# A decoder layer on one core: VectorE takes fourteen weight splits from GpSimd while it works on a small matrix inverse, and the table of delays that sets TensorE's order gets values for single steps

## The chip, the cores and the metric

The kernel runs on one core of a Trainium2 chip. The metric is the device time of one execution in microseconds (us). Engines are named as the profile names them: PE is TensorE, DVE is VectorE, ACT is ScalarE, POOL is GpSimd, SP is SyncE, the engine that here issues most of the transfers.

## The reference, cut to what matters

One decoder layer on x of 512 x 1024 in float32. All products are computed to float32 accuracy.

```python
h = rms_norm(x, pre_mix_norm)
proj = h @ w_in                      # 1024 -> 3600 columns: att q,k,v; gdn q,k,v,z,a,b
o_att = moba_attention(att_q, att_k, att_v, rel_bias)      # 8 heads of 64
# gated_deltanet: 8 heads, chunks of 64; q, k, v go through a causal conv of width 4 and silu
m = where(strict, (k_beta @ k.T) * decay, 0); a_mat = m + eye(64)
u, w = triangular_solve(a_mat, [v * beta, k_beta * exp(g_cum)])
def step(state, ...):                # lax.scan over the 8 chunks
    v_new = u_c - w_c @ state
    o = q_c @ state + attn_intra @ v_new
    state = state * exp(g_last) + k_c.T @ v_new
x = x + rms_norm(concat(o_att, o_gdn) @ w_out, post_mix_norm)
h = rms_norm(x, pre_mlp_norm)
x = x + rms_norm(square(relu(h @ w_up)) @ w_down, post_mlp_norm)
```

## The kernel before

Every large product is made of three: an operand is split into a high part (a cast to the type that PE multiplies at full rate) and a low part (operand minus high part), and hi·hi, hi·lo and lo·hi are added in PSUM (`mm3`). A weight of the input projection is handled in pieces of 128 x 512, two to a group of 128 output columns. For a piece, SP issues the load into `w_raw` (two buffers), ACT casts it to `w_hi` (three buffers), and POOL subtracts, which gives `w_lo` (three buffers): `begun` and `ended`, lines 128 to 140. A `w_raw` is free again when its `w_lo` is made, a `w_hi` when PE has used it.

`ORDER` lists the groups of columns: x, y are attention's queries and keys, w its values, k, q, v, z those of the delta net. A group takes 24 products of 128 x 512 (two pieces, four times three products each) into one of two PSUM banks named `ps_mm`; then its take-over starts (`take_k`, `take_q`, `take_v`, `take_z`, `take_a`), which evicts the bank on ACT and DVE. For a v group it is one ACT instruction, three DVE instructions `conv` at L395, a tanh (`th`), the product `vt` at L399, four transposes on PE and two DVE products into `vB`. A group's bank is free after its third `conv`. This text numbers the pieces as the program does: v0 has pieces 26 and 27, v1 28 and 29, v2 30 and 31, v3 32 and 33, y1 34 and 35, x2 36 and 37, y2 38 and 39, x3 40 and 41. By this time PE also does parts of the attention: scores of a pair of heads (`ps_a<-pt`), transposes (`ps_a<-ident,L`) and products with the values (`ps_a<-ph,V`).

`inverse` (L753 to L773) inverts the 32 x 32 diagonal blocks of all chunks on DVE: 31 steps of two instructions each, `pr` (L766) and `inv` (L767), each step on the result of the one before, then a copy (L770). The result goes through DRAM: `d_u<-inv` and `d_t<-inv` write it, and `scan` (L776 on) loads it in another layout, `uap<-d_t` and `UT<-d_u`, after POOL has set `UT` to zero (L778). Two products with 32 x 32 tiles follow (`ps_g<-uap,NT` and `ps_g<-UT,uap`), then `UT,kB`, and then the eight steps of the scan.

Tiles named "big" share 14 slots. A new one gets a slot that came free, and its first writer waits for the slot's last user. `UT`, `inv` and the scores' operands `pt` are such tiles.

What sets the order: each part of the work is a Python generator. `Weave` runs them against a clock of its own that counts the products' time alone; a generator that has to wait for other engines yields a delay, or marks a name with a delay, and the delays stand in the table `WAIT`, found by the kind of the wait. So `WAIT`, with ranks (`RANK`) and a few starting times (`START`), decides in which order PE's instructions are written, and PE runs them in that order. The instructions of ACT, DVE, POOL and SP are put in order when the program is built, by a scheduler with a model of the engines. On the chip each engine and each queue then runs its list strictly in order.

## Time and profile before

| | |
|---|---|
| runs | 653.94 us median of 3 (653.29 to 654.62) |
| the profiled execution | 652.92 us, of it 651.1 us from the first to the last instruction |
| granted TensorE clock, mean | 0.985 |
| PE busy | 629.3 us (97%), 4359 instructions |
| DVE busy | 444.7 us (68%) |
| ACT busy | 359.9 us (55%) |
| POOL busy | 181.8 us (28%) |
| DMA | 113.16 MB, mean 174 GB/s |

The profiled execution is 1.02 us under the median of the runs shown. PE is said to be busy nearly all the time, but a product that runs at half clock counts as busy as well, so the rows of the granted clock have to be read beside the busy time. Up to about 270 us the kernel is the mixer (norm, projections, attention, delta net), then come the output projection and, from about 350 us, the MLP.

### The profile page before, as it was taken

What the parts mean: (1) busy time and instruction counts of PE and PEld (TensorE: products, weight loads), DVE (VectorE), ACT (ScalarE), POOL (GpSimd) and SP (SyncE); (2) the same over time, 40 slices, a digit from 0 to 9 for tenths busy, and PEclk for the clock granted to TensorE, in tenths of its full rate; (3) what the DMA queues carried; (4) which work ended last, traced back from release to release, by engine and by line L of the source; (5) the groups of instructions that cost most, each with busy time, mean ns of one, the idle gap of its engine ahead of it and who ended that gap; (6) DMA issues with size and microseconds to landing.
All of it is one profiled execution on the core that took longest, in us unless ns stands there. A gap on an engine that the chain in (4) does not pass through costs nothing.

```text
span 651.1 us, 11131 instructions
## 1 busy us (share of the span) xinstructions
PE 629.3 (97%) x4359; PEld 528.7 (81%) x4359; DVE 444.7 (68%) x619; ACT 359.9 (55%) x610; POOL 181.8 (28%) x219
## 2 busy tenths in 40 slices
PE   8999999997979999999999999999999999999995
PEld 7788787865856777688898899999998888887884
DVE  5557656698432365576664578887879888988776
ACT  6456675333364647654433576666565656665661
POOL 4465574423452333202402112311111330000002
PEclk9999999998997999999999999999999999999999
DMA  7232332413250211382368989899999999957503
GB/s 238 84 102 78 82 111 68 130 64 129 78 116 21 66 34 67 132 295 84 122 227 264 254 230 264 215 254 284 256 230 347 313 293 290 308 201 292 199 1 129
DMA packets 60341, 113.16 MB, mean 174 GB/s; under 512 B 15702, under 2 KB 34777, under 8 KB 59906
## 3 DMA queue, kind: packets, MB, share of 16 engines
q1 hardware_dynamic: 42594, 83.10, 36.6%
q0 software_dynamic: 17696, 29.36, 21.4%
q8 instruction: 34, 0.56, 0.3%
q14 instruction: 17, 0.14, 0.1%
HBM read 106.65 MB, written 35.15 MB: 218 GB/s over the span
## 4 chain that ended last, share of the span: by engine, by line
PE 82%; DVE 9%; POOL 2%; DMA 2%; ACT 2%; issue 1%; SPq 1%; DVEq 0%; POOLq 0%; ACTq 0%
PE ps_mm L80 41%; PE ps_g L80 24%; PE ps_a L80 14%; DVE inv L767 2%; DVE pr L766 2%; PE ps_a L84 1%; PE ps_g L84 1%; DMA wo_raw<-in_w_out 1%; DVE conv L395 1%; DMA xx<-in_x 1%; DMA UT<-d_u 1%; POOL w_lo L138 1%; DVE ma_l L114 0%; DVE xs L1021 0%; SPq L786 0%
## 5 line engine op out<-in xcount | busy, mean ns | idle before, releaser
L138 POOL TENSOR_TENSOR w_lo<-w_raw,w_hi 128x512 fp32r<-128x512 f32 x54 | 71.0, 1316 | 100.3 <-ACT w_hi L137 92.5
L113 ACT CAST wdh<-wd 128x1024 fp32r<-128x1024 f32 x53 | 55.9, 1054 | 52.0 <-PE ps_mm L80 23.5
L80 PE MATMUL ps_mm<-hT_h,w_hi 128*128 128x512 f32 (+1 forms) x192 | 79.8, 415 | 4.5 <-DVE conv L395 4.5
L114 DVE TENSOR_TENSOR u_l<-w,u_h 128x1024 fp32r<-128x1024 f32 x46 | 56.2, 1224 | 37.9 <-ACT u_h L113 37.9
L114 DVE TENSOR_TENSOR wdl<-wd,wdh 128x1024 fp32r<-128x1024 f32 x53 | 64.9, 1224 | 22.8 <-ACT wdh L113 22.7
L113 ACT CAST u_h<-w 128x1024 fp32r<-128x1024 f32 x46 | 47.9, 1046 | 57.1 <-PE ps_a L80 20.9
L80 PE MATMUL ps_mm<-hT_l,w_hi 128*128 128x512 f32 (+1 forms) x192 | 74.7, 389 | 0.3 <-DVE hT_l L114 0.3
L80 PE MATMUL ps_mm<-hT_h,w_lo 128*128 128x512 f32 (+1 forms) x192 | 74.4, 388 | 0.0
L1192 POOL DMA_DIRECT2D d_T<-in_w_down x32 | 33.1, 1044 | 147.4 <-DMA d_T<-in_w_down 94.2
L137 ACT CAST w_hi<-w_raw 128x512 fp32r<-128x512 f32 x56 | 34.7, 619 | 52.3 <-PE ps_mm L80 17.8
L80 PEld LDWEIGHTS ps_mm<-hT_h,w_hi 128*128 128x128 f32 x192 | 37.0, 193 | 16.8 <-issue 9.9
L171 POOL TENSOR_SCALAR s<-s 128x1 f32<-128x1 f32 x12 | 4.1, 345 | 156.5 <-DVE s L1387 107.4
L80 PE MATMUL ps_mm<-wdh,u_h 128*128 128x512 f32 x116 | 45.3, 390 | 0.0
L80 PE MATMUL ps_mm<-wdh,u_l 128*128 128x512 f32 x116 | 45.1, 389 | 0.0
L80 PE MATMUL ps_mm<-wdl,u_h 128*128 128x512 f32 x116 | 45.1, 389 | 0.0
L80 PEld LDWEIGHTS ps_mm<-hT_h,w_lo 128*128 128x128 f32 x192 | 36.8, 192 | 7.8
L80 PEld LDWEIGHTS ps_mm<-hT_l,w_hi 128*128 128x128 f32 x192 | 37.0, 193 | 6.0 <-DVE hT_l L114 0.6
L692 DVE CUSTOM_DVE_ANT_0 L<-ps_a,E 128x512 f32<-128x512 f32 (+3 forms) x32 | 14.4, 488 | 32.6 <-PE ps_a L80 32.6
L395 DVE SCALAR_TENSOR_TENSOR conv<-ps_mm,cw,conv 128x511 f32<-128x511 f32 (+2 forms) x36 | 26.8, 744 | 11.8 <-ACT conv L392 11.3
L114 DVE TENSOR_TENSOR u_l<-f,u_h 128x1024 fp32r<-128x1024 f32 x28 | 34.1, 1217 | 0.0
L80 PE MATMUL ps_g<-wdh,u_h 128*128 128x512 f32 x80 | 31.2, 390 | 0.4 <-DVE y L1366 0.4
L80 PE MATMUL ps_g<-wdl,u_h 128*128 128x512 f32 x80 | 31.1, 389 | 0.0
(453 smaller groups left out, 1799.1 us busy)
## 6 DMA issues: line engine op xcount, KB each, us to landing
d_T<-in_w_down POOLq DMA_DIRECT2D x48, 512.0 KB, 12.2
wd<-d_T SPq DMA_DIRECT2D x32, 512.0 KB, 6.2
w<-in_w_up SPq DMA_DIRECT2D x28, 512.0 KB, 7.7
wd<-in_w_down SPq DMA_DIRECT2D x24, 512.0 KB, 8.4
w_raw<-in_w_in SPq DMA_DIRECT2D x46, 256.0 KB, 2.6
wo_raw<-in_w_out SPq DMA_DIRECT2D x16, 256.0 KB, 2.8
d_T<-d_T POOLq DMA_DIRECT2D x8, 512.0 KB, 11.0
xx<-in_x SPq DMA_DIRECT2D x4, 512.0 KB, 5.0
```

The lines of the kernel that those rows point to most:

```text
L80: nc.tensor.matmul(o, l, r, **kw)
L84: nc.tensor.transpose(o, i, ident[:k, :k])
L113: nc.scalar.copy(hi, src)
L114: tt(lo, src, f32(hi), op=OP.subtract)
L137: nc.scalar.copy(hi, raw)
L138: (sub or tt)(lo, raw, f32(hi), op=OP.subtract)
L171: nc.gpsimd.tensor_scalar(r, ss, 1.0 / n, EPS, op0=OP.mult, op1=OP.add)
L395: stt(c[:, s:], p[:, :512 - s], cw[:, ft, j:j + 1], c[:, s:], op0=OP.mult, op1=OP.add)
L692: nc.vector.tensor_tensor_reduce(out=l, in0=s[hh][:, :w], in1=Es[hh][:, w - 1::-1], scale=1.0, scalar=3e38, op0=OP.add, op1=OP.min, accum_ ...
L766: tt(v, iN[:, 0:m, m:m + 1].to_broadcast([128, m, w]), iU[:, m:m + 1, m:32].to_broadcast([128, m, w]), op=OP.mult)
L767: tt(iU[:, 0:m, m:32], iU[:, 0:m, m:32], v, op=OP.subtract)
L1192: nc.gpsimd.dma_start(d_T[t][k], block(b, second)[k], accum_op=OP.add, max_dma_last_dim=1024)
```

## The change

Three things change. First, `load` for pieces 26 to 39 no longer gives POOL as the subtracting engine, so DVE makes these fourteen `w_lo`; the eight pieces of attention's values before them and the pieces from 40 on stay with POOL. Second, a lookup `wait[...]` replaces `WAIT[...]` everywhere: it counts how often a kind has been asked for and gives the value of `SINGLE` for that occurrence, if there is one. Third, some values of `WAIT`, `START` and one of `RANK` are others. The arithmetic is the same, and so are the numbers of products, loads and subtractions.

```diff
-RANK = {..., 'take': 3}
+SINGLE = {('h', 0): 3.8, ('inverse', 6): 2.02, ('state', 6): 3.71, ('row', 5): 0.98, ... ('conv_v', 1): 8.5}
+RANK = {..., 'take': 4}
...
-START = (5.5, 9.0, 17, 16, 30, 16.5)
+START = (5.5, 9.7, 18.5, 15.3, 30, 15.0)
+LO_DVE = (26, 40)
...
+class Delays(dict):
+    def __init__(self, kinds, single):
+        super().__init__(kinds)
+        self.single = single
+        self.count = {}
+    def __getitem__(self, kind):
+        n = self.count[kind] = self.count.get(kind, -1) + 1
+        return self.single.get((kind, n), super().__getitem__(kind))
...
+    wait = Delays(WAIT, SINGLE)
...
-        load = lambda n: end(begin(n))
+        load = lambda n: ended(begin(n), None if LO_DVE[0] <= n < LO_DVE[1] else nc.gpsimd.tensor_tensor)
...
-            yield WAIT["inverse"]
+            yield wait["inverse"]
```

The rows below are the program's order, engine by engine; line numbers after the change are 17 higher. DVE, the end of the inverse, before: the copy L770 ends it, and behind it stand the `conv` of v1 (L395).

```order
L767 TENSOR_TENSOR inv<-inv,pr 128x4x28
L766 TENSOR_TENSOR pr<-inv 128x87
L767 TENSOR_TENSOR inv<-inv,pr 128x3x29
L766 TENSOR_TENSOR pr<-inv 128x60
L750 TENSOR_TENSOR t_1636<-ps_a,t_1611 128x512
L767 TENSOR_TENSOR inv<-inv,pr 128x2x30
L766 TENSOR_TENSOR pr<-inv 128x31
L767 TENSOR_TENSOR inv<-inv,pr 128x31
L770 COPY inv<-inv 128x1024
L114 TENSOR_TENSOR ma_l<-t_1636,ma_h 128x512
L395 SCALAR_TENSOR_TENSOR conv<-ps_mm,cw,conv 128x511
```

The same place after the change: `w_lo` at L155 are pieces 32, 33 and 34, `conv` at L412 are those of v1 and then of v2.

```order
L155 TENSOR_TENSOR w_lo<-w_raw,w_hi 128x512
L783 TENSOR_TENSOR pr<-inv 128x112
L412 SCALAR_TENSOR_TENSOR conv<-ps_mm,cw,conv 128x511
L784 TENSOR_TENSOR inv<-inv,pr 128x4x28
L412 SCALAR_TENSOR_TENSOR conv<-ps_mm,cw,conv 128x510
L783 TENSOR_TENSOR pr<-inv 128x87
L466 TENSOR_TENSOR vB<-ps_g,beta 128x4x64 x2
L412 SCALAR_TENSOR_TENSOR conv<-ps_mm,cw,conv 128x509
L784 TENSOR_TENSOR inv<-inv,pr 128x3x29
L155 TENSOR_TENSOR w_lo<-w_raw,w_hi 128x512
L783 TENSOR_TENSOR pr<-inv 128x60
L416 SCALAR_TENSOR_TENSOR vt<-th,conv 128x512
```

The evictions of v1 have moved from behind the inverse to ahead of its last steps, and the splits of the pieces now stand between its steps.

SP, from the write of the inverse to the load of `UT`, before:

```order
L771 DMA d_u<-inv 128x1024
L772 DMA d_t<-inv 128x1024
L132 DMA w_raw<-in_w_in 128x512 x8
L783 DMA uap<-d_t 32x16x32 x4
L132 DMA w_raw<-in_w_in 128x512 x2
L675 DMA E<-d_e 128x512 x2
L786 DMA UT<-d_u 32x32x32 x4
```

And after:

```order
L788 DMA d_u<-inv 128x1024
L789 DMA d_t<-inv 128x1024
L149 DMA w_raw<-in_w_in 128x512 x2
L803 DMA UT<-d_u 32x32x32 x4
L149 DMA w_raw<-in_w_in 128x512 x3
L800 DMA uap<-d_t 32x16x32 x2
L149 DMA w_raw<-in_w_in 128x512
L800 DMA uap<-d_t 32x16x32 x2
L149 DMA w_raw<-in_w_in 128x512
L692 DMA E<-d_e 128x512 x2
```

The load of `UT` has moved ahead of eight weight loads. In the built program `UT` had the slot of the second pair's `pt` (of x1 and y1), which PE reads up to the last score of that pair; it now has the slot of `inv` itself, and the next `pt` (of x2 and y2) has the slot that `UT` had. POOL's zeroing of `UT` moves likewise.

POOL, before:

```order
L138 TENSOR_TENSOR w_lo<-w_raw,w_hi 128x512 x20
L820 TENSOR_TENSOR kB<-kdec,kbe 128x512
L835 MEMSET S_2378 128x512
L835 MEMSET S_2379 128x512
L821 TENSOR_TENSOR kdec<-kdec,kde 128x4x128
L138 TENSOR_TENSOR w_lo<-w_raw,w_hi 128x512
L778 MEMSET UT 128x2048
```

And after, where the first five `w_lo` are the last of attention's values:

```order
L155 TENSOR_TENSOR w_lo<-w_raw,w_hi 128x512 x5
L795 MEMSET UT 128x2048
L155 TENSOR_TENSOR w_lo<-w_raw,w_hi 128x512
L837 TENSOR_TENSOR kB<-kdec,kbe 128x512
L852 MEMSET S_2378 128x512
L852 MEMSET S_2379 128x512
L838 TENSOR_TENSOR kdec<-kdec,kde 128x4x128
```

Fourteen subtractions have left POOL's list, and the zeroing of `UT` follows the last one before them directly. On PE the groups of products keep their numbers and nearly their order; some ten groups of the attention and the delta net move by one to three steps of three products (0.68 us each) to a later or an earlier place.

## The prediction

> **What bounds the kernel now.** The page first: the span, the row of TensorE's granted clock, and the shares of the chain that ended last.

> ```profile
> span 651.1 us, 11131 instructions
> PEclk9999999998997999999999999999999999999999
> PE 82%; DVE 9%; POOL 2%; DMA 2%; ACT 2%; issue 1%; SPq 1%; DVEq 0%; POOLq 0%; ACTq 0%
> ```

> PE carries 82% of the chain, so time is to be had only where PE waits or runs slowly. A slice is 16.3 us. The clock dips in the tenth slice (147 to 163 us) and in the thirteenth (195 to 212). Second view, PE's waits, longest in total first:

> ```profile
> PE ps_mm L80 <- DVE conv L395: 4.5, 1, 4.5
> PE ps_g L80 <- DMA UT<-d_u: 4.2, 2, 3.2
> PE ps_a L84 <- DVE xs L1021: 1.1, 2, 0.7
> PE ps_g L84 <- DVE LWQ L592: 0.6, 1, 0.6
> ```

> All other waits of PE are shorter, most of them at the start. The two long ones have a second price, which the busy time by stretches shows (columns: stretch, its length, busy time and number of PE, PEld, DVE, ACT, POOL, granted clock, DMA):

> ```profile
> 153.70:158.26 4.56, 0.02 (x2) 0.03 (x1) 4.38 (x6) 0.54 (x2) 2.78 (x2) 0.81 0.82 301
> 158.26:163.40 5.14, 5.14 (x12) 4.08 (x13) 2.94 (x4) 1.70 (x4) 1.28 (x1) 0.50 0.17 60
> 191.84:195.03 3.19, 0.00 (x1) 0.03 (x1) 0.00 (x0) 1.72 (x4) 0.00 (x0) 0.86 0.74 89
> 195.03:200.00 4.97, 4.01 (x130) 3.84 (x132) 0.00 (x0) 1.28 (x3) 0.00 (x0) 0.50 0.29 77
> 200.00:204.36 4.36, 4.36 (x28) 2.47 (x30) 0.00 (x0) 1.83 (x4) 0.00 (x0) 0.50 0.00 0
> ```

> After each wait the granted clock is 0.50, for 5.14 us of PE's work in the first place and 4.01 + 4.36 = 8.37 us in the second. Half of it is lost: 2.6 and 4.2 us. So the first place costs 4.5 + 2.6 = 7.1 us, the second 4.2 + 4.2 = 8.4 us, together 15.5. The chain in order of time says what each waits for (start, length, what):

> ```profile
> 152.53 1.15 DVE inv L770
> 155.35 0.67 DVE conv L395
> 157.46 0.67 DVE conv L395
> 158.26 8.14 PE ps_mm L80 x24
> 166.83 5.47 PE ps_mm L80 x24
> ...
> 187.51 1.81 POOL UT L778
> 190.31 1.43 SPq L786
> 191.78 4.36 DMA UT<-d_u
> 196.27 3.58 PE ps_g L80 x126
> ```

> The 24 products from 158.26 are v3's. They need the bank that v1 had, and v1's `conv` stand behind the inverse's copy on DVE, so v3 starts when the third ends (158.13). The 8.14 against 5.47 us for the next 24 is the halved clock. The second place starts with `UT` being set to zero at 187.51, although the inverse had ended 34 us earlier.

> **Why the inverse ends so late.** DVE's and POOL's timeline, and the splits of the output weights as the price of a split on DVE:

> ```profile
> 127.48 0.39 DVE L766 TENSOR_TENSOR pr<-inv 128x220 f32<-128x220 f32 x1
> 128.32 1.43 DVE L766 TENSOR_TENSOR pr<-inv 128x231 f32<-128x231 f32 x1
> 129.79 0.40 DVE L767 TENSOR_TENSOR inv<-inv,pr 128x231 f32<-128x231 f32 x1
> 144.88 0.74 DVE L395 SCALAR_TENSOR_TENSOR conv<-ps_mm,cw,conv 128x511 f32<-128x511 f32 x1
> 125.48 1.32 POOL L138 TENSOR_TENSOR w_lo<-w_raw,w_hi 128x512 fp32r<-128x512 f32 x1 [0.81 <-ACT w_hi L137]
> 128.20 1.30 POOL L138 TENSOR_TENSOR w_lo<-w_raw,w_hi 128x512 fp32r<-128x512 f32 x1 [1.40 <-ACT w_hi L137]
> 131.36 1.32 POOL L138 TENSOR_TENSOR w_lo<-w_raw,w_hi 128x512 fp32r<-128x512 f32 x1 [1.86 <-ACT w_hi L137]
> L126 DVE TENSOR_TENSOR wo_l<-wo_raw,wo_h x16: 680/688/980, 251.4 to 284.2; 128x512 fp32r<-128x512 f32 x16
> ```

> The `pr` that starts 0.12 us after POOL's `w_lo` takes 1.43 us and ends just after it; its `inv` twin of the same size takes 0.40. So a `w_lo` on POOL holds DVE for about 1.0 us, and on DVE it takes 0.69.

> **The change part by part.**

> *The splits.* Pieces 26 to 31 are split by POOL inside the inverse today and hold it for 6 x 1.0 = 6.0 us; the two pieces of attention's values at its start stay with POOL. In the new list nine pieces, 26 to 34, stand ahead of the copy: 9 x 0.62 (0.69, of which some 0.07 lies under the next instruction's start) = 5.6 us. That alone leaves the inverse's length as it is. But the three `conv`, `vt` and `vB` of v1, two `conv` of v2 and `ma_l` have moved in as well, 9 instructions for about 5 us, so by this account the inverse ends near 153.7 - 6.0 + 5.6 + 5 = 158.3, later than today. That costs PE nothing as long as `UT` has slack, below.

> *v3's wait.* What matters is when v1's third `conv` ends. v0's first `conv` is at 144.88 today, behind five pieces on POOL (5.0 us); now it stands behind five on DVE (3.1) and three steps earlier in the inverse (2.2): 140.8. From there to v1's third the new list has seven instructions of `conv` and `vt` (0.74 in the row, some 0.08 of it under the next: 4.6), two pieces (1.25), two products of `vB` of half that size (0.7), `t` and `ma_l` at a piece's price (1.3) and thirteen of the inverse with 220 falling to 87 elements (0.39 at 220, 0.32 on the mean: 4.1), and by my estimate a wait for the tanh (0.3): 12.3, that is 153.1. PE ends v2 at 153.7 today and will be no earlier than 153.1. I take a remaining wait of 0.4 us for v3; with it the clock has no cause to fall. Bounds: 0, and 3.5 us where every piece comes 0.5 us late (seven stand ahead). Gain 7.1 - 0.4 = 6.7.

> *The scan's start.* `UT` now waits for `d_u` and `d_t` alone.

> ```profile
> d_t<-inv SPq DMA_DIRECT2D x1, 512.0 KB, 2.9
> UT<-d_u SPq DMA_DIRECT2D x4, 128.0 KB, 5.2
> w_raw<-in_w_in SPq DMA_DIRECT2D x19, 256.0 KB, 2.5
> ```

> 158.3 + 0.3 + 2.9 (landing) + 1.8 (zeroing) = 163.3, four issues of up to 1.43 us, 5.2 to land: 168 to 174. PE reaches the first product with `UT` at 191.84 today less the first place's 7.1, so at 185; eleven us of slack hide the later inverse. `uap` now follows more weight loads on SP: its last part is issued after piece 42, which I put at 175 (POOL's split of piece 40, whose load is held by DVE's split of 38 at 167, plus two loads of 2.5 and their casts), and lands at 179 with PE there at 181. Two us of slack: here the cover is thin. The weight loads that `UT` has passed on SP, pieces 39 to 41, wait for up to 5 us; y2's second half needs piece 39 at about 175, and it lands by 171. DVE's scores stand behind its split. I allow 0.5 for all this and keep 8.4 - 0.5 = 7.9. Bounds: 8.4, and 8.4 - 4.2 if the clock falls all the same.

> *The steps moved by the delays.* The transposes that waited 0.6 us for `LWQ` move 1.4 us back and lose the wait; the two transposes that waited 1.1 for `xs` L1021 both move back by 0.7 us or more: 1.7 gained in all. Some ten other groups move, several of them to an earlier place, by 1.4 us at most. The first is the transposes of `kraw`, which DVE ends at 32.28 and PE starts at 34.49 today, so they keep 0.9 us of slack:

> ```profile
> 31.66 0.62 DVE L399 SCALAR_TENSOR_TENSOR kraw<-th,conv 128x512 f32<-128x512 f32 x1
> 34.49 0.60 PE L84 MATMUL ps_g<-ident,kraw 128*128 128x128 f32 x4
> ```

> The others I can't clear one by one. Ten new waits at the 0.6 us of the old ones would be 6, none would be 0; I take as many as go, three, and so 1.7. START and RANK move nothing else on PE.

> The sum: 6.7 + 7.9 + 1.7 - 1.7 = 14.6 us. The profiled execution's 652.92 becomes 638.3; the median of the runs shown stands 1.0 above it, so I predict 639.3. What follows, from 205 us on, is PE's work with waits that hang on PE's own progress, and moves as a block.

> [...] The second halving of the clock came 2.3 us after PE had stopped (0.86 over 3.19 us at 1.0 or 0.5 means 0.9 us halved), the first 2.8 us after. [...]

> **The rivals.**

> *The clock falls at the scan's start all the same.* The 4.2 us come back: 643.5. For it: 128 tiny products stand on both sides of that place. Against: every other slice of the page's row is at 9, those with many small products from 212 to 260 us too.

> *The splits come late, a little.* DVE runs in order, so a piece whose `w_hi` isn't there holds the inverse and v1's `conv`. At 0.5 us a piece v3 waits 3.5, and the clock may halve again (2.6): 642.5 to 645.

> *They come late by much: slower.*

> ```profile
> POOL w_lo L138 <- ACT w_hi L137: 25.3, 10, 8.6
> ```

> This row is of 118 to 154 us: POOL waited 25.3 us for ten casts, 2.5 each. If DVE inherits these waits, v1's third `conv` comes 7 x 2.5 = 17.7 us later, v3 waits that long instead of 4.5, and with the clock halved as before the first place loses 13.3 us and the gains of the second (7.9) remain: 5 us slower, 659. It decides from 2.0 us a piece. Against: POOL had nothing else to do. From the end of a split to the start of the next but one it took 131.36 - 126.80 = 4.56 us, the turn of one of the two `w_raw`; in the new list two pieces are 4.7 us of DVE's own work apart, so the cast should be there.

> *Nothing is gained.* PE's 97% were the limit, and each wait that goes turns up at the next bank: 652 to 655. Against: the clock's loss is no wait, and PE has no other wait over 1 us after 12 us.

> **How the numbers follow.** My forecast, both places mended, 637 to 642: 0.62. The clock alone comes back, 643.5: 0.12. Splits somewhat late, 642.5 to 645: 0.14. Slower, about 659: 0.07. No gain: 0.05. The low end takes all bounds at their best (15.5 + 1.7 = 17.2, 636.7) with 1 us for the scatter of the runs: 635.5. The high end takes the late splits with another 2 us of short waits (645 + 2): 647. Together they hold 0.88. A measurement of this kernel can tell 0.2%, 1.3 us, from no change. Faster by more: 0.62 + 0.12 + 0.14 = 0.88, and a part of no gain, 0.01; within: 0.04; slower: 0.07.

> **What would show it.** In the new profile: no `pr` or `inv` over 0.6 us except beside POOL's two remaining pieces early on; v1's third `conv` near 153 and ahead of the copy; the wait for `conv` under 1 us and none for `UT`; the clock's row without a dip from the tenth to the thirteenth slice; the copy L787 near 158 and `UT` zeroed about 5 us later. The prediction is wrong if DVE shows idle time ahead of its `w_lo`, if PE waits for `uap` or for a `ps_mm` bank, or if the clock is at 0.50 after the first 32 x 32 products.

## The result and the profile after

The changed kernel takes 636.47 us (median of 4, 635.4 to 637.33) against 654.28 of before (median of 4, 653.29 to 654.98): ratio 0.9728, interval 0.9707 to 0.9749, 17.8 us. The forecast was 639.3 within 635.5 to 647. The profiled execution took 637.33 us, 635.2 of it from the first to the last instruction; line numbers are 17 higher than before. Of the experiments below, one execution of e9 (two more buffers for `E`) took 1020.78 us and one of before beside it 879.3 us, at granted clocks of 0.561 and 0.658; the ratios leave both out, the medians have them.

The page first, with the three lines that were read of before:

```profile
span 635.2 us, 11133 instructions
PEclk9999999999999999999999999999999999999998
PE 89%; DVE 3%; ACT 3%; DMA 2%; POOL 1%; issue 1%; SPq 0%; DVEq 0%; POOLq 0%; ACTq 0%
```

The clock's row has no dip left before its last slice; DVE has gone from 9% to 3% of the chain and PE from 82% to 89%. PE's waits, longest first:

```profile
PE ps_g L101 <- DVE xs L249: 1.1, 2, 0.6
PE ps_g L97 <- DVE rb L202: 1.1, 1, 1.1
PE ps_g L97 <- DVE y L1383: 0.4, 1, 0.4
```

The waits for `conv` (4.5) and `UT` (4.2) are gone, and so are those for `xs` L1021 (1.1; the one above is another, at the kernel's start) and `LWQ` (0.6). The busy time by stretches (columns as before), at v3's first products and around the 32 x 32 products, with the clock at 1.00 in every row:

```profile
154.45:159.60 5.15, 5.15 (x26) 4.29 (x25) 4.72 (x12) 2.31 (x4) 0.00 (x0) 1.00 0.63 236
181.90:185.22 3.32, 3.32 (x140) 2.94 (x139) 0.69 (x1) 3.25 (x7) 1.22 (x1) 1.00 0.61 190
185.22:189.62 4.40, 4.40 (x146) 3.45 (x145) 0.00 (x0) 4.07 (x9) 0.00 (x0) 1.00 0.04 9
```

DVE's, POOL's and SP's timeline through the inverse (start, length, what, in brackets the idle time ahead):

```profile
121.30 1.25 DVE L784 TENSOR_TENSOR inv<-inv,pr 128x112 f32<-128x112 f32 x1
124.36 1.46 POOL L155 TENSOR_TENSOR w_lo<-w_raw,w_hi 128x512 fp32r<-128x512 f32 x1 [1.94 <-ACT w_hi L154]
124.71 1.32 DVE L783 TENSOR_TENSOR pr<-inv 128x192 f32<-128x192 f32 x1
128.88 0.69 DVE L155 TENSOR_TENSOR w_lo<-w_raw,w_hi 128x512 fp32r<-128x512 f32 x1
140.70 0.74 DVE L412 SCALAR_TENSOR_TENSOR conv<-ps_mm,cw,conv 128x511 f32<-128x511 f32 x1
149.17 0.69 DVE L155 TENSOR_TENSOR w_lo<-w_raw,w_hi 128x512 fp32r<-128x512 f32 x1 [0.36 <-ACT w_hi L154]
152.29 0.74 DVE L412 SCALAR_TENSOR_TENSOR conv<-ps_mm,cw,conv 128x509 f32<-128x509 f32 x1
157.23 1.11 DVE L787 COPY inv<-inv 128x1024 f32<-128x1024 f32 x1
161.27 1.81 POOL L795 MEMSET UT<- 128x2048 f32 x1 [35.45 <-DMA d_t<-inv]
163.11 2.74 SPq L803 DMA_DIRECT2D UT<-d_u  x4
174.15 0.95 SPq L800 DMA_DIRECT2D uap<-d_t  x2
```

The only `pr` and `inv` over 0.6 us stand beside POOL's two remaining pieces. v1's third `conv` ends at 153.03, ahead of the copy, which ends at 158.34; `UT` is set to zero from 161.27 on, when `d_t<-inv` has landed.

For all that follows one table is used. It cuts each profiled execution at the starts of certain products on PE, and each column is the time from the cut before it: A up to the second halves of the first two groups, B to v0, C to v3, D to the first 32 x 32 product, E to the first product with `UT`, F to the first `UT,kB`, G to the output projection, H to the end (us). A wait for `conv` and the slow clock after it stand in C and D, a wait for `UT` and what follows it in E and F.

| kernel | A | B | C | D | E | F | G | H |
|---|---|---|---|---|---|---|---|---|
| before | 24.09 | 105.89 | 28.28 | 30.20 | 6.58 | 8.99 | 71.93 | 375.15 |
| before, useless products | 23.68 | 105.98 | 28.32 | 27.74 | 6.99 | 5.17 | 71.76 | 375.18 |
| rank alone | 24.83 | 105.85 | 28.28 | 29.30 | 3.32 | 7.20 | 72.33 | 375.44 |
| rank, E buffers | 25.92 | 106.25 | 28.31 | 29.28 | 3.32 | 4.78 | 71.88 | 375.18 |
| splits alone | 25.25 | 106.02 | 23.54 | 27.66 | 6.36 | 8.48 | 71.99 | 375.16 |
| splits, rank | 25.52 | 105.90 | 23.54 | 27.66 | 3.32 | 7.40 | 72.04 | 375.15 |
| splits, rank, E buffers | 23.63 | 106.04 | 23.54 | 27.66 | 3.32 | 4.78 | 72.06 | 375.18 |
| splits, rank, two delays | 24.75 | 105.89 | 23.54 | 27.45 | 3.32 | 4.40 | 73.00 | 375.18 |
| changed, splits on POOL | 26.01 | 105.12 | 29.25 | 29.62 | 3.32 | 4.39 | 70.88 | 374.03 |
| changed, without two delays | 25.59 | 104.97 | 23.59 | 27.66 | 3.32 | 6.00 | 71.12 | 374.08 |
| changed | 25.77 | 105.09 | 23.59 | 27.45 | 3.32 | 4.40 | 71.19 | 374.40 |
| changed, again | 26.72 | 105.62 | 23.59 | 27.45 | 3.32 | 5.21 | 71.26 | 374.32 |
| changed, E buffers | 23.24 | 106.26 | 23.59 | 27.45 | 3.32 | 4.66 | 70.94 | 373.83 |
| changed, values on DVE | 24.24 | 105.15 | 23.59 | 27.45 | 3.32 | 4.41 | 71.06 | 374.31 |

A varies from 23.6 to 25.9 us among seven kernels with the same list of PE there as before, so a single profile's span tells nothing below 2 us. B varies by 1.3 us among the kernels with the changed list (105.0 to 106.3); the other columns repeat to some tenths wherever the same thing is done. From before to the changed kernel C + D give 7.4, E + F 7.9, and B, G and H together 2.3 (1.7 to 3.6 over all pairs of a profile with the old order there and one with the new).

### The profile page after: what moved, and what is told of

Same layout as the page of the kernel before. It is cut to its first block, busy times and chain, and to the rows that moved or that the text cites. A ratio compares the mean times of both kernels' runs of the same rounds, so it can differ in the third digit from the quotient of the medians.

```text
span 635.2 us, 11133 instructions
## 1 busy us (share of the span) xinstructions
PE 624.3 (98%) x4359; PEld 526.2 (83%) x4359; DVE 443.2 (70%) x633; ACT 359.0 (57%) x610; POOL 162.1 (26%) x205
## 4 chain that ended last, share of the span: by engine, by line
PE 89%; DVE 3%; ACT 3%; DMA 2%; POOL 1%; issue 1%; SPq 0%; DVEq 0%; POOLq 0%; ACTq 0%
PE ps_mm L97 44%; PE ps_g L97 26%; PE ps_a L97 16%; PE ps_a L101 2%; PE ps_g L101 1%; DMA wo_raw<-in_w_out 1%; DMA xx<-in_x 1%; DVE conv L412 1%; DMA w_raw<-in_w_in 0%; POOL oss L192 0%; ACT wdh L130 0%; DVE wo_l L143 0%; ACT u_h L130 0%; DVE hT_l L131 0%; ACT wo_h L142 0%
## 5 line engine op out<-in xcount | busy, mean ns | idle before, releaser
L155 POOL TENSOR_TENSOR w_lo<-w_raw,w_hi 128x512 fp32r<-128x512 f32 x40 | 52.2, 1307 | 77.4 <-ACT w_hi L154 67.9
L412 DVE SCALAR_TENSOR_TENSOR conv<-ps_mm,cw,conv 128x511 f32<-128x511 f32 (+2 forms) x36 | 26.8, 745 | 11.7 <-ACT conv L409 11.3
## 6 DMA issues: line engine op xcount, KB each, us to landing
d_T<-in_w_down POOLq DMA_DIRECT2D x48, 512.0 KB, 11.4
wd<-d_T SPq DMA_DIRECT2D x32, 512.0 KB, 6.2
w<-in_w_up SPq DMA_DIRECT2D x28, 512.0 KB, 8.1
wd<-in_w_down SPq DMA_DIRECT2D x24, 512.0 KB, 7.1
w_raw<-in_w_in SPq DMA_DIRECT2D x46, 256.0 KB, 2.8
wo_raw<-in_w_out SPq DMA_DIRECT2D x16, 256.0 KB, 3.3
d_T<-d_T POOLq DMA_DIRECT2D x8, 512.0 KB, 11.8
xx<-in_x SPq DMA_DIRECT2D x4, 512.0 KB, 4.9
```

What stands on the lines that cost most here:

```text
L155: (sub or tt)(lo, raw, f32(hi), op=OP.subtract)
L412: stt(c[:, s:], p[:, :512 - s], cw[:, ft, j:j + 1], c[:, s:], op0=OP.mult, op1=OP.add)
```

## The experiments

The first four take the change apart. The order of instructions shows two of its parts to be separable: the splits on DVE alone leave PE's list as it was, and so does the rank of `take`, which alone decides which slot `UT` gets.

**The splits back on POOL**, in the changed kernel (e1):

```diff
-LO_DVE = (26, 40)
+LO_DVE = (0, 0)
```

> The changed kernel with all weight splits back on POOL; its tables stay, PE's list is word for word the changed kernel's. On DVE the three conv of v1 stand behind the inverse's copy again. Theory (each of the two places carries a wait and a halved clock, and the splits on DVE mend the first alone): v3 waits about 4.5 us for conv again, the clock halves for about 5 us, UT's load stays early and PE does not wait for it; 7.1 us above the changed kernel, 643.6. Rival (the tables do it all, the splits are only moved work): within 1 us of the changed kernel, 636 to 637. [...]

Measured: 642.84 us, ratio 0.9847 (0.9824 to 0.9869). v3 waits again, and the clock falls; PE's wait, then the busy time by stretches:

```profile
PE ps_mm L97 <- DVE conv L412: 5.5, 1, 5.5
```

```profile
154.90:160.38 5.48, 0.00 (x0) 0.03 (x1) 5.20 (x9) 0.05 (x1) 1.24 (x2) 0.78 0.58 204
160.38:165.50 5.12, 5.12 (x15) 4.02 (x16) 2.94 (x4) 2.01 (x4) 3.07 (x2) 0.57 0.67 152
```

C and D are 5.7 and 2.2 us longer than in the changed kernel, E and F the same. So the splits on DVE carry the first place, and the table of delays does not mend it.

**The splits alone**, in the kernel before (e2): `load` with `LO_DVE = (26, 40)`, nothing else.

> The kernel before, with the splits of pieces 26 to 39 on DVE and nothing else; PE's list is word for word that of before, UT keeps its late slot. Theory: v1's conv come ahead of the copy, v3's wait and its halved clock go, the scan's start keeps its wait for UT (4.2) and its halved clock (4.2): 654.3 - 7.1 = 647.2, between 646.5 and 648.5. Rival (without the new delays DVE is late with the splits): no gain, 653 to 656. Rival (PE comes earlier to the scan and just waits longer for UT, whose slot hangs on DMA and POOL): the first place's gain is given back, 652 to 654.

Measured: 646.08 us against 653.0 beside it, 6.9 us less, ratio 0.9891 (0.987 to 0.9912). The wait for `conv` is gone; the one for `UT` stays, and of the 8.5 us behind its first part 6.8 pass at half clock (0.60 in the mean). PE's wait, then the stretches:

```profile
PE ps_g L81 <- DMA UT<-d_u: 4.1, 2, 3.0
```

```profile
185.86:188.84 2.98, 0.01 (x2) 0.04 (x2) 0.00 (x0) 1.72 (x4) 0.00 (x0) 1.00 0.79 101
188.84:193.78 4.94, 3.80 (x130) 3.65 (x132) 0.00 (x0) 1.17 (x2) 0.00 (x0) 0.60 0.28 71
193.78:197.32 3.54, 3.54 (x17) 1.81 (x17) 0.00 (x0) 1.50 (x3) 0.00 (x0) 0.60 0.00 0
```

The first place is worth what the theory said, without any new delay, and PE's earlier arrival is not given back at `UT`, since POOL's zeroing came earlier with it.

**The rank alone**, in the kernel before (e3):

```diff
-RANK = {..., 'take': 3}
+RANK = {..., 'take': 4}
```

> The kernel before with the rank of take 4 instead of 3 and nothing else; PE's list is word for word that of before, but UT gets the slot of inv and its load stands ahead of eight weight loads. Theory: the first place stays as it was (4.5 us of wait, clock at 0.50 after it), the second goes with its halved clock: 654.3 - 8.4 = 645.9, between 645 and 647. Rival (the halving at the scan's start comes from the 32 x 32 products and not from the wait): 4.2 us only, 650.1. Rival (the slot is worth nothing without the earlier inverse): 653 to 655.

Measured: 648.87 us, 4.1 less, ratio 0.993 (0.9909 to 0.995), and not 8.4. The wait for `UT` is gone, but something else stops PE among the products with `UT`, and the clock falls after it. PE's waits, its timeline and a stretch:

```profile
PE ps_mm L80 <- DVE conv L395: 4.6, 1, 4.6
PE ps_g L80 <- issue: 1.1, 1, 1.1
```

```profile
191.58 1.96 PE L80 MATMUL ps_g<-UT,uap 32*32 32x32 f32 x88
194.66 0.82 PE L80 MATMUL ps_g<-UT,uap 32*32 32x32 f32 x40 [1.12 <-issue]
```

```profile
195.48:198.78 3.30, 3.30 (x16) 1.99 (x17) 0.00 (x0) 1.76 (x3) 0.00 (x0) 0.63 0.03 5
```

"issue" is a wait for nothing that the profile names. The first reading of this was the rival, that the tiny products themselves let the clock fall; the kernels further down contradict it.

**The splits and the rank**, in the kernel before (e4).

> The kernel before with both the splits on DVE and the rank of take, all other delays and starting times as before; PE's list is word for word that of before. Theory (the two places add): 654.3 - 7.1 - 8.4 = 638.8, between 638 and 640, about 2 us above the changed kernel, whose other delays would be worth those 2 us. Rival (the single delays carry more, because DVE's splits need the groups moved): over 641. Rival (the other delays only cost, as the later start of the inverse in the changed kernel suggests): 636 or less.

Measured: 642.24 us, 10.8 less, ratio 0.9822 (0.9798 to 0.9846). The two parts add (6.9 + 4.1 = 11.0), and 3 us or more lie in the other delays, more than I had put there. The stop is at the same place: after 88 of the 128 products, 0.93 us in which PE waits for nothing that the profile names, then the clock at 0.50. PE's lists of e3 and e4 are those of before. Stretches of e4:

```profile
187.91:188.84 0.93, 0.00 (x1) 0.00 (x1) 0.00 (x0) 0.91 (x3) 0.00 (x0) 1.00 0.00 0
188.84:190.11 1.27, 1.27 (x46) 1.08 (x47) 0.00 (x0) 0.84 (x2) 0.00 (x0) 1.00 0.05 13
190.11:193.35 3.24, 3.24 (x15) 1.73 (x11) 0.00 (x0) 1.34 (x3) 0.00 (x0) 0.50 0.00 0
```

**What stops PE.** The profile lists a DMA queue, q8, with the kind "instruction": in e4 34 packets and 0.56 MB, blocks of 16 KB. In e4's DMA view of 184 to 186.6 us there is none, and the DMA engines carry data for 67.6% of the time, then run dry; the next 1.1 us hold one block. Two answers of that view (DMA share in 40 slices of the window, GB/s, queues):

```profile
DMA  6989889999598699696749778577544431200000
DMA packets 336, 0.60 MB, mean 229 GB/s; under 512 B 45, under 2 KB 45, under 8 KB 336
q1 hardware_dynamic: 336, 0.60, 67.6%
...
DMA packets 2, 0.02 MB, mean 15 GB/s; under 512 B 1, under 2 KB 1, under 8 KB 1
q8 instruction: 1, 0.02, 5.5%
```

The block starts at 186.67, when the data are through; PE stops at 187.91 and goes on 1.2 us after the block's end. The data are two loads of `E` (2 x 256 KB) and a weight piece that SP issues at 181.95 and 182.99, from 0.7 us ahead of the first 32 x 32 products. In the changed kernel the loads of `E` are issued 1.8 us ahead of them, and the block starts at 184.40, before the products with `UT`. So the new theory: those products, with their weight loads, use up instructions so fast (89 products and 89 loads in the 1.97 us before the stop in e4) that PE runs out of them where the next block waits behind data. The place bears it out. In all four profiles with the stop (e3, e4, and e5 and e10 below) PE stands still ahead of the same product, the 89th with `UT`, and goes on 1.20 to 1.37 us after the end of the same block (the ninth in each profile). Where PE neither stops there nor waits for `UT` first, that product comes 1.27 us (changed kernel) to 1.67 us (e9) after the block's end, so the changed kernel has next to nothing to spare. Two of the single delays, `('row', 5)` and `('row', 6)`, end the second pair's scores earlier and so free `E` earlier. Three kernels test it.

**The changed kernel without these two delays** (e5).

> The changed kernel without two single delays, (row, 5) and (row, 6). PE's list differs in one place: six projection products of 128 x 512 that stand right ahead of the six transposes before the first 32 x 32 products go back between the scores. Theory (those scores end earlier in the changed kernel, so the loads of E come earlier, and a block of PE's instructions that is fetched over the same DMA engines arrives in time): without them the block comes late again, PE stops about 1.1 us among the second 32 x 32 products with no releaser, and the clock halves for one record of 3.4 us (1.7 us lost): 3 us above the changed kernel, ratio to before 0.977. Rival (six products moved by 2 us change nothing): ratio 0.973, as the changed kernel.

Measured: 638.19 us, ratio 0.9772 (0.9757 to 0.9787). The stop is back, though the clock stays up in the profiled execution:

```profile
PE ps_g L97 <- issue: 1.0, 1, 1.0
```

```profile
185.13:188.95 3.82, 2.64 (x131) 2.37 (x132) 0.00 (x0) 3.23 (x7) 0.00 (x0) 1.00 0.06 21
188.95:191.13 2.18, 2.18 (x17) 1.28 (x16) 0.00 (x0) 1.50 (x3) 0.00 (x0) 1.00 0.03 8
```

F is 1.6 us longer than in the changed kernel. The ratio lies above the first one of the changed kernel, but a later set of runs of that kernel gave 0.9776 as well (below), so it is the trace and not the ratio that decides here: without the two delays the stop is there. The halved clock does not follow from every such stop.

**The kernel of e4 with only these two delays** (e8): 0.98 and 0.38 us for the second and third step of the second pair.

> The kernel before with the splits on DVE, the rank of take and only two delays of the new table, 0.98 and 0.38 us for the second and third step of the second pair's scores. Theory (these two keep the instruction block from being late): 3 us faster than the same kernel without the two delays, whose ratio was 0.982: 0.977, and the remaining 0.4% to the changed kernel lies in small waits elsewhere. Rival (the stall goes with the other delays): 0.982.

Measured: 638.52 us, ratio 0.9784 (0.9764 to 0.9803); no stop, and F is 4.40 against 7.40. The expected 3 us are in that column; between the ratios lie 2.5 us, with intervals that just overlap.

**Two more buffers for `E`**, in the kernel of e4 (e9), which moves nothing but the issue of these loads:

```diff
-                E = at.tile([128, 512], FT, name="E")
+                E = at.tile([128, 512], FT, name="E", tag="E" if p < 2 else "E2")
```

> The kernel before with the splits on DVE and the rank of take, and with two more buffers for E, so that the loads of E for the last two pairs are not issued about 1 us before the first 32 x 32 products; the lists of PE, DVE, ACT and POOL are word for word the same as without the buffers. Theory (the late instruction block waits behind these loads, 2 x 256 KB, on the DMA engines): the block's fetch starts about 1.5 us earlier, the stop of 1.1 us among the second 32 x 32 products goes, the clock stays up: about 3 us faster than without the buffers, ratio 0.977. Rival (the stop has to do with the order of PE's instructions and not with the loads): ratio 0.982 and the stop stays.

Measured: 640.21 us, ratio 0.98 (0.9779 to 0.9821), 2 us less than e4 by the medians, with intervals that overlap; the trace is plainer, F 4.78 against 7.40. The block starts at 183.34, 0.85 us ahead of the first product with `UT`, on DMA engines with little else to do, and there is no stop (DMA view of 183.3 to 184.4, then two stretches):

```profile
DMA packets 6, 0.02 MB, mean 19 GB/s; under 512 B 3, under 2 KB 3, under 8 KB 5
q8 instruction: 1, 0.02, 5.5%
```

```profile
184.19:186.79 2.60, 2.45 (x131) 2.30 (x132) 0.00 (x0) 2.53 (x6) 0.00 (x0) 1.00 0.00 0
186.79:188.97 2.18, 2.18 (x17) 1.27 (x16) 0.00 (x0) 2.10 (x5) 0.00 (x0) 1.00 0.03 8
```

PE's list is word for word that of e4, so the order of products is not the cause: the loads are, by when they are issued.

**The rank alone with the two buffers** (e12).

> The kernel before with the rank of take and two more buffers for E, no split moved and no delay changed; PE's, DVE's lists as with the rank alone. Theory (the second place is worth its whole 8 us once the instruction block is in time too): no wait for UT, no stop among the second 32 x 32 products, clock at 1.0 there; 3 us faster than the rank alone (0.993), ratio 0.988. Rival (the rest of the second place's price is not the block): 0.993.

Measured: 645.31 us, ratio 0.989 (0.9871 to 0.9909), 2.6 us below the rank alone by the ratios, whose intervals touch. F is 4.78 against 7.20, the clock is at 1.00, and only v3's wait for `conv` (4.6) is left of the two places. With the block in time the second place gives 7.5 us in E and F (6.9 between the medians), close to its price of 8.4.

**Useless products in the two waits**, in the kernel before (e6): 18 ahead of v3, 16 ahead of the products with `UT`.

> The kernel before with useless products of 128 x 512 in its two long waits: 18 ahead of v3 (3.9 us) into a bank that the next transposes overwrite, and 16 ahead of the first products with UT (3.4 us) into the bank that these overwrite. Nothing else is changed and no wait is shortened. Theory (the waits have a second price, the halved clock after them): the clock stays at 1.0 in both places, 2.6 + 4.2 us are won, 6.8 us faster than before, ratio 0.990. If only the first place is saved (since at the second a late instruction block and tiny products halve the clock too): 2.6 us, ratio 0.996. Rival (the halving is set by something else than PE's idleness): no gain, ratio 1.000 or a little above.

Measured: 650.69 us, ratio 0.9954 (0.9936 to 0.9972), but its executions spread from 646.65 to 652.21. The profiled one is the fastest: 644.8 us of span, 6.3 less than before, although PE did 34 products more and waited for the same things. Its stretches at the two places:

```profile
157.90:163.00 5.10, 5.01 (x22) 4.22 (x23) 3.17 (x5) 2.62 (x5) 1.30 (x1) 1.00 0.23 79
192.72:195.71 2.99, 2.43 (x131) 2.30 (x132) 0.00 (x0) 0.89 (x2) 0.00 (x0) 1.00 0.20 73
```

The clock is at 1.00 where it was at 0.50. By the columns, which leave A's scatter out, 2.5 us are won in D and 3.4 in E and F together, 5.9 of the 6.8 expected. So the second price is real and is paid for PE standing still. The median won only 2.3 us, and why is open: in five of the twelve executions the mean granted clock was 0.992 or less, and they took 651.0 to 652.2 us, the others 646.65 to 651.1, but only one was profiled, and a mean does not say where the clock fell (in e10 below it is 0.988, for a loss in the first 19 us).

**The changed kernel again, with the two buffers, and with the last two value pieces on DVE** (e10, e11, e13), on one chip.

> The changed kernel itself once more, so that the next kernels have it on the same chip. Theory: ratio 0.973 as at first.

> The changed kernel with two more buffers for E; the lists of all compute engines stay. Theory (its two score delays already bring the instruction block in time): no difference, within 0.2% of the changed kernel. Rival (other blocks or loads are still late behind E): 1 us or more faster, ratio 0.971 or less.

> The changed kernel with the splits of the last two value pieces on DVE too, so that POOL has none inside the inverse; PE's list stays. Theory (nothing on PE waits for the inverse any more): DVE's two stretched instructions (1.25 and 1.32 us) go, v1's third conv ends up to 0.7 us earlier, and the time stays within 0.2% of the changed kernel. Rival (an earlier inverse is still worth its time): 1 us faster or more, ratio 0.971 or less.

Measured: 637.58 us, 0.9776 (0.9756 to 0.9796); 635.94, 0.975 (0.973 to 0.977); 635.45, 0.9741 (0.9722 to 0.9759). The changed kernel came out 0.5% nearer to before than at first, beyond its interval; before itself took 2.0 us less in this set of runs (652.24 against 654.28) and the changed kernel 1.1 more, and the cause is open. Its profile has the longest A of all, with the clock at 0.50 from 8.15 to 18.39 us, and the stop again, 0.6 us, where the block took 1.9 us instead of 1.0; 0.23 MB of data moved beside it, as beside that of the changed kernel's first profile. PE's wait, then the DMA view of 185.7 to 187.6:

```profile
PE ps_g L97 <- issue: 0.6, 1, 0.6
```

```profile
DMA packets 130, 0.25 MB, mean 132 GB/s; under 512 B 15, under 2 KB 15, under 8 KB 129
q8 instruction: 1, 0.02, 6.2%
```

So even the changed kernel has this cover only by a little. With the buffers there is no stop, and 1.6 us less by medians with overlapping intervals: unclear, as is the 2.1 us of the values. For these two, columns C to E are to the hundredth those of the changed kernel, and PE has no wait there that hangs on the inverse. With the values on DVE v1's third `conv` did not end earlier against v0's start than in the changed kernel (22.2 us in both), as two splits waited 0.68 and 0.63 us for their casts. Most of the difference between the spans of e10 and e13 (637.5 and 633.5) lies in A (2.5) and F (0.8).

## Why the prediction was right

*The first place.* Forecast 6.7, measured 7.4 (C 4.7, D 2.7; 7.3 with the splits alone). The mechanism was the forecast one. v0's first `conv` was put at 140.8 and came at 140.70, v1's third at 153.1 and came at 153.03, the copy's end at 158.3 and came at 158.34. That these agree to 0.1 us is in part luck: in this profile the inverse starts at 119.41 and v0 at 130.85, in that of before at 118.61 and 129.98, and counted from there DVE was 0.8 to 1.0 us faster than forecast. The stretch from v0's first `conv` to v1's third was right (12.3 forecast and measured). The price of a split inside the inverse was too high: 0.62 was taken, but from an `inv` to the next `pr` it is 0.92 us with a split between them and from a `pr` to its `inv` 0.43 without one, so a split adds about 0.5. That is 0.6 less for the five splits ahead of v0's first `conv`; the rest is that the three steps which it passed took 2.5 us before (142.17 to 144.62), not 2.2.

```profile
128.13 0.40 DVE L783 TENSOR_TENSOR pr<-inv 128x231 f32<-128x231 f32 x1
128.56 0.40 DVE L784 TENSOR_TENSOR inv<-inv,pr 128x231 f32<-128x231 f32 x1
129.48 0.40 DVE L783 TENSOR_TENSOR pr<-inv 128x240 f32<-128x240 f32 x1
```

So v1's third `conv` ended 22.2 us after v0's start, v3 followed 23.6 us after it, and the remaining wait of 0.4 us did not occur. The rival that casts would be late stayed small: DVE waited 0.36 and 0.43 us ahead of two splits up to the copy. Taken by the letter this is one of the prediction's own signs of being wrong, but no wait of PE came of it.

*The second place.* Forecast 7.9, measured 7.9, by a way that the prediction did not know. It took an early `UT` for enough. The rank, which sets the slot, gives only 5.1 by itself (E 3.3, F 1.8; e3), because the rival of the clock that falls all the same comes true there, together with a stop of 1.1 us that the prediction had no term for. The other 2.8 come from two single delays (3.0 where they were added alone, e8; 1.6 where they were taken away, e5, whose profile kept its clock). Their six moved products stood among the groups that the prediction could not clear one by one, so that the whole 7.9 was reached is luck as far as the prediction goes. `UT` was zeroed 161.27 to 163.08 and its load issued from 163.11, forecast 163.3; `uap` was issued by 175.1 and did not make PE wait.

*The moved steps.* Here the sum was mis-sized: 1.7 gained less 1.7 for three new waits made 0, and B, G and H measured 2.3. The waits that went were there (0.6, 1.1, and 0.5 and 0.3 at transposes that wait for `ph` and `om`, 2.5 in all), and new ones hardly came. One of the doubted kind did in e11: the transposes of `kraw`, given 0.9 us of slack, waited 1.2 us, and in e10 0.6 us.

```profile
PE ps_g L101 <- DVE kraw L416: 1.2, 1, 1.2
```

In all, 14.6 was forecast, and 7.4 + 7.9 + 2.3 = 17.6 was measured in these columns, against 17.8 between the medians. Of the missing 3.0 us, 2.3 are the moved steps, and 0.7 is the first place, 0.4 of it the wait of v3 that was not there.

## What to carry to other kernels

Here two waits of PE were worth fifteen us: their length, 4.5 and 4.2 us, and half of the 5.1 and 8.4 us at half clock after them; read the granted clock behind each wait before pricing it. Where hundreds of tiny products follow each other, look at the instruction blocks among the DMA queues: keep large loads from being issued just ahead of them, by another buffer or an earlier release (2.6 and 3.0 us of F here). And take a profile apart at fixed points of PE's list before comparing spans, since the first 25 us alone vary by two.

## What was not expected of the hardware

The profile's instruction queue moves 34 blocks of 16 KB in an execution (0.56 MB), and the one behind 0.6 MB of loads came about 1.5 us later (start 186.67 in e4 against 183.34 in e9, whose PE reaches that place 1.8 us earlier); in e4 PE stood still for 0.93 us there and went on 1.2 us after the block's end.
